# Hybrid mLSTM/Hyena block: step 0 of the MLP's first product is written between the last row tiles of the output projection

## The chip, the core and the metric

The kernel runs on one core of a Trainium2 chip. Its engines each follow their own instruction stream: TensorE (PE in the profile, matmuls and transposes), VectorE (DVE), ScalarE (ACT), GpSimd (POOL) and SyncE (SP, which here only starts DMA transfers). The time is that of one execution on the device in microseconds (us). For the kernel before it was measured three times: 2784.33, 2786.06 and 2790.24 us, median 2786.06.

## The reference

One encoder block over 2048 rows of width 1024. A mixing part (mLSTM heads and a Hyena operator) gives `y`, and then:

```python
x = x + rms_norm(y @ w_out, norm_mix_post)
hm = rms_norm(x, norm_mlp_pre)
ff = jnp.square(jax.nn.relu(hm @ w_mlp_in)) @ w_mlp_out
x = x + rms_norm(ff, norm_mlp_post)
```

`w_mlp_in` is 1024 x 4096 and `w_mlp_out` 4096 x 1024. Everything is float32.

## The kernel before

Only two stages matter here, the output projection and the first product of the MLP.

**Numbers in two parts.** A float32 operand of a matmul is held as a part hi, which ScalarE makes by a cast (L166), and a remainder lo, which VectorE or GpSimd makes by a subtraction (L169). One product of two operands takes three matmuls, hi and lo crossed (L159, L160, L161).

**The output projection** (`out_proj`, L1269) works on 16 row tiles of 128 rows in 18 turns of a loop. A turn i makes the operands of later row tiles, multiplies row tile i with `w_out` in two halves of 512 columns, and then runs `finish(i)`: the post norm (squares of `po` on ScalarE at L1198, the scaling on VectorE at L1204, the residual add on GpSimd at L1205), the store of the new rows, and the next norm (square L1333, root L1334, scale L1336). Two turns later `turn_out` transposes the normalized tile on TensorE (L1346), multiplies it with the norm's weight on VectorE (L1347), and stores what the MLP needs to DRAM (`ht`). For every second row tile GpSimd first forms the sums and differences of L1361 to L1364. Row tile 15 is thus finished in turn 15 and transposed in turn 17, the last.

**The first product of the MLP** (`up`, L1524) saves multiplications: a product of 2 x 2 blocks is computed with 7 smaller products instead of 8, from sums of blocks. The rows come in two halves, 0 (row tiles 0 to 7) and 1 (8 to 15), and the weights in 16 blocks, which gives 32 steps; steps 0 to 15 are half 0. A step computes its products in the order 1, 2, 6, 5, 7, 4, 3. Each is 12 matmuls (4 blocks of depth, three matmuls each), so a step is 84 matmuls, and ends in a PSUM bank, from which ScalarE copies it (product 1, L1561) or VectorE adds it up (L1539); relu and square are done on ScalarE (L1543, L1544) and results stored to DRAM (`ga`).

Product i of half h takes the operand `hm[i]`, which `right(h, i)` (L1470) loads from `ht` in two pieces of 512 KB, each split into hi and lo: the lo of the first piece is VectorE's, of the second GpSimd's. Weights of step s come from `up_weights(s)` (L1441): two loads, then four sums on GpSimd (L1452, L1453, L1456, L1458) with splits between them, whose hi parts are ScalarE's and lo parts GpSimd's. Operands 1 and 2 of half 0 and the weights of step 0 are prepared by `first_operands` during turns 11 to 14 and later of the output projection. Operands 6, 5, 7, 4 and 3 are loaded at the start of the MLP.

**What sets the order.** Inside the loop of the output projection and throughout the MLP, TensorE, VectorE and ScalarE follow the order of the code; GpSimd and SyncE are ordered by a scheduler within their dependencies. A tile of a pool waits for the last user of the place it takes. The pools of the output projection (`owp` with the weights `wo` and `wbo`, `owk` with its scratch) are closed after its last turn, and the pools of the MLP take their place.

A load goes through SyncE's queue and a store through ScalarE's, so that a store that waits for its data holds the ScalarE instructions behind it.

Of the kernel before, what the change touches and what calls it, by code (L numbers as in the profile page):

```python
# [17 lines left out]
D = 1024  # L18
# [129 lines left out]
class Builder:  # L148
# [95 lines left out]
    def build(self):  # L244
        tc, nc = self.tc, self.nc
        with ExitStack() as c:
# [66 lines left out]
            oc = ExitStack()  # L313
            out = self.out_proj(oc)
# [5 lines left out]
            self.hm_pool = {i: hp for i in (1, 2)}  # L320
# [4 lines left out]
            oc.close()  # L325
# [867 lines left out]
    def post(self, wk, src, wb, tmp, res, tag):  # L1193
# [8 lines left out]
        for e in range(2):  # L1202
            cs = slice(512 * e, 512 * e + 512)
            self.dve.scalar_tensor_tensor(tmp[e], src[e], r, wb[:, cs], ALU.mult, ALU.mult)  # L1204
            self.pool.tensor_tensor(res[:, cs], tmp[e], res[:, cs], ALU.add)  # L1205
# [63 lines left out]
    def out_proj(self, c):  # L1269
        tc, io = self.tc, self.io  # L1270
        pe, dve, act, pool = self.pe, self.dve, self.act, self.pool
        wp = c.enter_context(tc.tile_pool(name="owp", bufs=1))
        wk = c.enter_context(tc.tile_pool(name="owk", bufs=2))
        ps = c.enter_context(tc.tile_pool(name="opt", bufs=3, space=PSUM, side="right"))
        pp = c.enter_context(tc.tile_pool(name="opo", bufs=3, space=PSUM, side="right"))
        wo = [wp.tile([128, 8, D], F32R, name=f"wo{e}") for e in range(2)]
        wb = wp.tile([128, D], F32, name="wbo")
# [7 lines left out]
        def weight(k):  # L1285

            wf = ahead.pop(k)
            act.activation(wo[0][:, k, :], wf, AF.Copy, scale=yw[:, k:k + 1])
            dve.scalar_tensor_tensor(wo[1][:, k, :], wf, yw[:, k:k + 1], wo[0][:, k, :].bitcast(F32),
                                     ALU.mult, ALU.subtract)  # L1290
# [13 lines left out]
        def turned(src, tag):  # L1304
            y = [wk.tile([128, 4, 128], F32R, tag=f"{tag}{e}", name=f"{tag}{e}") for e in range(2)]
            self.turn_split(ps.tile([128, 512], F32, tag="tp", name="ptp", bufs=3), src, y)
            return y
# [10 lines left out]
        def part(po, e, y, k0):  # L1318
            cs = slice(512 * e, 512 * e + 512)
            for k in range(4):  # L1320
                self.mm3(po[e], (y[0][:, k, :], y[1][:, k, :]), (wo[0][:, k0 + k, cs], wo[1][:, k0 + k, cs]),
# [5 lines left out]
        def finish(h, po):  # L1327
            xt = wk.tile([128, D], F32, tag="xt", name="xt")
            self.load(xt, self.rows(io["x"][0], h))
            x1 = wk.tile([128, D], F32, tag="xo", name="xo", bufs=3)  # L1330
            self.post(wk, po, wb, (x1[:, 0:512], x1[:, 512:1024]), xt, "po")
            self.store(self.x1[h], xt)
            act.activation(x1, xt, AF.Square, accum_out=ss1[:, h:h + 1])  # L1333
# [46 lines left out]
        yz[1] = turned(zs.pop(1), "yhz")  # L1380
# [3 lines left out]
        ym = {0: turned(mixed(0), "yhm")}  # L1384
# [7 lines left out]
        for i in range(18):  # L1392
            with tc.manual_schedule(engines={mybir.EngineType.PE,mybir.EngineType.DVE,mybir.EngineType.Activation}):
                if i == 0:
# [3 lines left out]
                    ym[1] = turned(ys.pop(1), "yhm")  # L1398
# [3 lines left out]
                if 0 < i < 15:  # L1402
                    yz[i + 1] = turned(zs.pop(i + 1), "yhz")
# [7 lines left out]
                if 0 < i < 15:  # L1411
                    ym[i + 1] = turned(ys.pop(i + 1), "yhm")
# [80 lines left out]

    def mlp(self):
        tc, io = self.tc, self.io
        pe, dve, act, pool = self.pe, self.dve, self.act, self.pool
        with ExitStack() as c:
            hp = c.enter_context(tc.tile_pool(name="hmq", bufs=1))
            mk = self.mk = c.enter_context(tc.tile_pool(name="mmk", bufs=1))
            self.mwp = c.enter_context(tc.tile_pool(name="mwp", bufs=2))  # L1500
            ps = c.enter_context(tc.tile_pool(name="mlps", bufs=2, space=PSUM, side="right"))
            self.hm_pool.update({i: hp for i in (3, 4, 5, 6, 7)})
            self.wb2 = mk.tile([128, D], F32, name="wb2")
# [20 lines left out]
    def up(self, ring, next_bank, down):  # L1524
# [12 lines left out]

        def add(dst, a, b):
# [7 lines left out]
        w = self.w1_first  # L1546
        nxt = weights(1)
        for i in (6, 5, 7, 4, 3):
            self.right(0, i, staging, (None, pool))
        for s in range(n):  # L1550
            half, turn = s // 16, s == 15
            ga = self.ga[s % 16, half]
            gt = [ring((128, 2, 512), 0) for _ in range(2)]
            (c11, c12), (c21, c22) = [[t[:, b] for b in range(2)] for t in gt]
            for i in (1, 2, 6, 5, 7, 4, 3):
                pt = next_bank()
                hi, lo = self.hm[i]
                for k in range(4):
                    self.mm3(pt, w(i, k), (hi[:, k, :], lo[:, k, :]), k == 0, k == 3)
                if i == 1:  # L1560
                    act.copy(c11, pt)  # L1561
                elif i == 2:
                    p2 = pt
                    if s + 1 < n:
                        w1 = next(nxt)
                    if s + 2 < n:
                        nxt = weights(s + 2)
                elif i == 6:
                    add(c22, pt, c11)
                    add(c11, p2, c11)  # L1570
                    square(c11)
                elif i == 5:
                    add(c12, pt, c22)
                    p5 = pt
                elif i == 7:
                    add(c21, pt, c22)
                    add(c22, p5, c21)
                    square(c22)
                elif i == 4:
                    add(c21, pt, c21)  # L1580
                    square(c21)
                    self.store(ga[:, 2:4, :], gt[1])
                else:
# [234 lines left out]
```

## Time and profile before

| | |
|---|---|
| median of three runs | 2786.06 us (2784.33 to 2790.24) |
| profiled execution, its own time | 2789.98 us |
| its span, first to last instruction | 2787.9 us |
| mean granted clock of TensorE | 0.973 |
| last transposes of row tile 14 end | 1490.2 us after the span's start |
| first matmul of step 0 of the MLP | 1506.42 us |

A row of the timeline gives the start, the duration, the engine, the line and operation, what is written and read (tiles by their names), how many instructions the row holds, and in brackets how long the engine stood idle before it and what ended the wait. A row of waits gives engine, tile and line, what was waited for, the total, the count and the longest. A row of the windows gives for one stretch the busy time of each engine, the granted clock and the share of the DMA engines in use. A row of groups gives the busy time and mean duration of one kind of instruction.

### The profile page before, as it was taken

Reading aid. Unit: us, or ns where it says so; the run is one execution under the profiler, and the core shown is the slowest. Engines: PE = TensorE matmul, PEld = TensorE weight load, DVE = VectorE, ACT = ScalarE, POOL = GpSimd, SP = SyncE. Lnnn points to the kernel's source line nnn. Section 1 sums busy time; section 2 is a strip of 40 time slices with the busy share of each in tenths; the row PEclk is TensorE's granted clock in tenths of the full one; section 3 lists DMA queues with packets and bytes.
Section 4 is the critical chain, followed back from the end, with each engine's and each line's share of the span. In section 5 each row is a group of like instructions: output and inputs, shape, how many; then the busy total and the mean of one; then the engine's idle time right before and its main releaser. Section 6 shows DMA issues by size and latency. Waiting matters only on the chain. (4 is left out here: it accounts for less than half of the span.)

```text
span 2787.9 us, 35849 instructions
## 1 busy us (share of the span) xinstructions
PE 2617.9 (94%) x12422; PEld 2140.6 (77%) x12422; DVE 1530.7 (55%) x2593; ACT 1223.3 (44%) x2237; POOL 1199.6 (43%) x946
## 2 busy tenths in 40 slices
PE   6999999999899998888996999989999999999998
PEld 5778877777677888776775788868888888888876
DVE  5676643777436664664443454564445443443478
ACT  6355543655434444543332445455445233232244
POOL 1221124554215542424565877777774251310232
PEclk8999999999999999999998999989999999999999
DMA  6233346565556656955665444464445653444546
GB/s 168 61 99 106 106 138 201 183 194 169 189 192 176 186 164 227 267 187 187 212 214 198 143 159 143 156 223 141 157 159 201 222 181 114 113 144 153 194 152 226
DMA packets 307189, 474.24 MB, mean 170 GB/s; under 512 B 37814, under 2 KB 166198, under 8 KB 305984
## 3 DMA queue, kind: packets, MB, share of 16 engines
q1 hardware_dynamic: 231952, 333.24, 38.4%
q10 hardware_dynamic: 70304, 125.98, 12.1%
q0 software_dynamic: 4752, 12.72, 2.1%
q8 instruction: 99, 1.62, 0.2%
q14 instruction: 82, 0.67, 0.1%
HBM read 297.65 MB, written 174.20 MB: 169 GB/s over the span
## 5 line engine op out<-in xcount | busy, mean ns | idle before, releaser
L166 ACT CAST cb<-m 128x1024 fp32r<-128x1024 f32 (+1 forms) x346 | 281.8, 850 | 446.4 <-PE pm L159 385.7
L169 DVE TENSOR_TENSOR cb<-m,cb 128x1024 fp32r<-128x1024 f32 (+1 forms) x222 | 238.9, 1113 | 300.4 <-ACT cb L166 290.6
L159 PE MATMUL pm<-hm,cb 128*128 128x512 f32 x896 | 354.4, 396 | 15.0 <-issue 8.3
L160 PE MATMUL pm<-hm,cb 128*128 128x512 f32 x896 | 353.8, 395 | 13.3 <-POOL hm L169 9.6
L161 PE MATMUL pm<-hm,cb 128*128 128x512 f32 x896 | 352.4, 393 | 0.0
L160 PE MATMUL pm<-cb 128*128 128x512 f32 x880 | 343.9, 391 | 6.4 <-DVE cb L169 6.4
L159 PE MATMUL pm<-cb 128*128 128x512 f32 x880 | 342.7, 390 | 1.0 <-DVE cb L169 1.0
L161 PE MATMUL pm<-cb 128*128 128x512 f32 x880 | 343.1, 390 | 0.0
L169 POOL TENSOR_TENSOR cb<-m,cb 128x1024 fp32r<-128x1024 f32 x124 | 270.4, 2193 | 53.4 <-ACT cb L166 53.4
L1539 DVE TENSOR_TENSOR m<-pm,m 128x512 f32<-128x512 f32 x224 | 154.0, 690 | 243.3 <-PE pm L161 232.5
L159 PE MATMUL pt<-hn,w 128*128 128x512 f32 x640 | 270.9, 423 | 1.0 <-ACT hn L486 0.9
L169 POOL TENSOR_TENSOR raw<-raw,hi 128x512 fp32r<-128x512 f32 x160 | 205.4, 1296 | 129.5 <-ACT hi L166 118.3
L160 PE MATMUL pt<-hn,w 128*128 128x512 f32 x640 | 254.9, 398 | 0.3 <-DVE hn L487 0.2
L161 PE MATMUL pt<-hn,w 128*128 128x512 f32 x640 | 253.6, 396 | 0.0
L159 PEld LDWEIGHTS pm<-hm,cb 128*128 128x128 f32 x896 | 171.0, 191 | 53.2 <-issue 10.0
L160 PEld LDWEIGHTS pm<-hm,cb 128*128 128x128 f32 x896 | 171.0, 191 | 51.4 <-POOL hm L169 11.3
L160 PEld LDWEIGHTS pm<-cb 128*128 128x128 f32 x880 | 165.6, 188 | 43.8 <-DVE cb L169 9.4
L161 PEld LDWEIGHTS pm<-hm,cb 128*128 128x128 f32 x896 | 171.0, 191 | 35.5
L159 PEld LDWEIGHTS pm<-cb 128*128 128x128 f32 x880 | 165.4, 188 | 35.9 <-ACT junk L1728 1.4
L161 PEld LDWEIGHTS pm<-cb 128*128 128x128 f32 x880 | 165.6, 188 | 34.1
L1543 ACT ACTIVATE m<-m 128x512 f32<-128x512 f32 x128 | 80.5, 630 | 219.6 <-DVE m L1539 211.7
L630 POOL DMA_DIRECT2D vp<-vst x96 | 61.2, 642 | 236.4 <-ACT vst L626 235.1
(323 smaller groups left out, 5699.0 us busy)
## 6 DMA issues: line engine op xcount, KB each, us to landing
ga<-m ACTq DMA_DIRECT2D x96, 512.0 KB, 3.8
m<-ga SPq DMA_DIRECT2D x96, 512.0 KB, 3.7
d<-st ACTq DMA_DIRECT2D x64, 512.0 KB, 3.3
m<-in_w_mlp_in_dram SPq DMA_DIRECT2D x62, 512.0 KB, 4.6
m<-in_w_mlp_out_dram SPq DMA_DIRECT2D x114, 256.0 KB, 4.0
raw<-d SPq DMA_DIRECT2D x96, 256.0 KB, 2.8
xt<-in_x_dram SPq DMA_DIRECT2D x32, 512.0 KB, 5.6
dk<-kst SPq DMA_DIRECT2D x32, 512.0 KB, 3.3
```

Of the source, the lines that this page charges most:

```text
L159: pe.matmul(ps, w[1], x[0], start=first, stop=False)
L160: pe.matmul(ps, w[0], x[1], start=False, stop=False)
L161: pe.matmul(ps, w[0], x[0], start=False, stop=last)
L166: self.act.copy(hi, src)
L169: (eng_lo or self.dve).tensor_tensor(lo, src, hi.bitcast(F32), ALU.subtract)
L630: pool.dma_start(dst[:, 8 * b + e:8 * b + 8:2, cc:cc + 128], st[64 * e:64 * e + 64])
L1539: dve.tensor_tensor(dst, a, b, ALU.add)
L1543: act.activation(g, g, AF.Relu)
```

## The change

Four things are done. **One pool for both stages**: the pool `hmq` of the MLP's operands is opened before the output projection, whose weights take the places of operands 6, 5, 7 and 4, and whose turned tiles those of operand 3; `wbo` and `wb2`, the weights of the two post norms, share one place. The scratch pool is closed after turn 14, and a small pool `m0` takes its room. **Step 0 moves**: `first_step`, a generator, emits the loads of operands and the seven products of step 0 in turns 15 to 17; the code of a step is now `up_step`, and the MLP starts at step 1. **The norm of row tile 15**: `finish` is cut in two, `finish` and `normed`, so that operand loads can stand between them, and the residual add of row tile 15 is on VectorE instead of GpSimd. **Pools of the MLP** wait tile by tile for their places (`reuse_waits="tile"`).

```diff
+            self.hq = c.enter_context(tc.tile_pool(name="hmq", bufs=1))
+            self.hm_pool = {i: self.hq for i in range(3, 8)}
             out = self.out_proj(oc)
...
-            oc.close()
             self.mlp()
...
-            self.pool.tensor_tensor(res[:, cs], tmp[e], res[:, cs], ALU.add)
+            eng.tensor_tensor(res[:, cs], tmp[e], res[:, cs], ALU.add)
...
-        wp = c.enter_context(tc.tile_pool(name="owp", bufs=1))
-        wk = c.enter_context(tc.tile_pool(name="owk", bufs=2))
+        wp = self.hq
+        wl = c.enter_context(tc.tile_pool(name="owl", bufs=2))
+        gc = ExitStack()
+        wk = gc.enter_context(tc.tile_pool(name="owk", bufs=2))
...
-        wo = [wp.tile([128, 8, D], F32R, name=f"wo{e}") for e in range(2)]
-        wb = wp.tile([128, D], F32, name="wbo")
+
+        wos = {j: [wp.tile([128, 2, D], F32R, tag=f"hm{i}{e}", name=f"wo{e}") for e in range(2)]
+               for j, i in ((2, 6), (3, 5), (0, 7), (1, 4))}
+        wo = [[wos[k // 2][e][:, k % 2, :] for k in range(8)] for e in range(2)]
+        wb = wp.tile([128, D], F32, tag="wb", name="wbo")
...
-                if i < 16:
+                if i < 15:
                     part(pos[i], 1, ym[i], 0)
-                    xns[i] = finish(i, pos.pop(i))
-            if i > 10:
-                next(staged, None)
+                    xns[i] = normed(i, *finish(i, pos.pop(i)))
+                elif i == 15:
+
+                    part(pos[i], 1, ym[i], 0)
+                    step = self.first_step(c, pp)
+                    next(step)
+                    rows = finish(i, pos.pop(i))
+                    next(step)
+                    xns[i] = normed(i, *rows)
+                    next(step)
+                elif i == 16:
+                    for _ in range(4):
+                        next(step)
+                else:
+                    for _ in step:
+                        pass
+            if 10 < i < 15:
+                next(staged)
+            if i == 14:
+                gc.close()
             yield
-        for _ in staged:
-            pass
+        c.close()
...
+    def first_step(self, c, pp):
+
+        wk = c.enter_context(self.tc.tile_pool(name="m0", bufs=1))
+        count = [0]
+
+        def tile(shape, tag):
+            return wk.tile(list(shape), F32, tag=tag, name="m0", bufs={"g": 3, "s": 1, "r": 4}[tag])
+
+        def staging():
+            return tile((128, 2, 512), "r")
+
+        def bank():
+            count[0] += 1
+            if count[0] in (1, 2, 4, 5):
+                return self.h1p.tile([128, 512], F32, tag="h1", name="pm")
+            return pp.tile([128, 512], F32, tag="po", name="pm", bufs=3)
+
+        def then(i):
+            if i == 1:
+                self.right(0, 4, staging, (None, self.pool))
+            elif i == 2:
+                self.w1 = next(nxt)
+            elif i == 6:
+                self.right(0, 3, staging, (None, self.pool))
+
+        self.right(0, 6, staging, (None, self.pool))
+        yield
+        self.right(0, 5, staging, (None, self.pool))
+        yield
+        nxt = self.up_weights(1, [tile((128, 4, 256), "r") for _ in range(2)], tile((128, 2, 4, 128), "r"))
+        next(nxt)
+        self.right(0, 7, staging, (None, self.pool))
+        yield
+        yield from self.up_step(0, self.w1_first, lambda: tile((128, 2, 512), "g"), lambda: tile((128, 512), "s"), bank, then)
+
...
-            self.wb2 = mk.tile([128, D], F32, name="wb2")
+            self.wb2 = self.hq.tile([128, D], F32, tag="wb", name="wb2")
...
+        w1, nxt = self.w1, weights(2)
+        for s in range(1, n):
+            for _ in self.up_step(s, w1, lambda: ring((128, 2, 512), 0),
+                                  lambda: self.mk.tile([128, 512], F32, tag="mc", name="m4"), next_bank, then):
+                pass
```

How the order moves is seen at three places. In these rows `hm61` is the lo part of operand 6 and so on, `m` and `m0` are staging tiles and partial results, `cb` parts of weights, `pm` PSUM banks of products, `po` those of the output projection, `xo` and `xt` row tiles.

The first place is SyncE's queue after the last row tile of x has been asked for. Before:

```order
L231 DMA xt_14348<-in_x_dram 128x1x1024
L231 DMA wb2_14429<-in_norm_mlp_post_dram 128x1024
L231 DMA m_14431<-in_w_mlp_in_dram 128x4x256
L231 DMA m_14432<-in_w_mlp_in_dram 128x4x256
L231 DMA m_14438<-ht_84 128x1024
L231 DMA m_14442<-ht_84 128x1024
L231 DMA m_14448<-ht_84 128x1024
```

and of the changed kernel:

```order
L231 DMA xt_14325<-in_x_dram 128x1x1024
L231 DMA m0_14317<-ht_84 128x1024
L231 DMA m0_14321<-ht_84 128x1024
L231 DMA m0_14344<-ht_84 128x1024
L231 DMA m0_14348<-ht_84 128x1024
L231 DMA m0_14356<-in_w_mlp_in_dram 128x4x256
L231 DMA m0_14357<-in_w_mlp_in_dram 128x4x256
L231 DMA wb2_14586<-in_norm_mlp_post_dram 128x1024
L231 DMA m0_14363<-ht_84 128x1024
L231 DMA m0_14367<-ht_84 128x1024
L231 DMA m0_14406<-ht_84 128x1024
L231 DMA m0_14410<-ht_84 128x1024
```

The four loads of operands 6 and 5 moved ahead of the weights of step 1 and of wb2, whose place is that of `wbo`; those of 7 and 4 stand behind them.

The second place is VectorE from the post norm of row tile 15 to the first evacuation of step 0. Before:

```order
L1204 SCALAR_TENSOR_TENSOR xo_14350<-po1_14276,po_r_14358,wbo_12116 128x512
L1335 RECIPROCAL r1_12118<-ss1_12117 128x1
L1336 TENSOR_SCALAR xo_14350<-xt_14348,r1_12118 128x1024
L1347 TENSOR_TENSOR xo_14350<-pto_14389,nw1_3589 128x512
L1347 TENSOR_TENSOR xo_14350<-pto_14395,nw1_3589 128x512
L169 TENSOR_TENSOR hm61_14437<-m_14438,hm60_14436 128x1024
L169 TENSOR_TENSOR hm51_14447<-m_14448,hm50_14446 128x1024
L169 TENSOR_TENSOR hm71_14457<-m_14458,hm70_14456 128x1024
L169 TENSOR_TENSOR hm41_14467<-m_14468,hm40_14466 128x1024
L169 TENSOR_TENSOR hm31_14477<-m_14478,hm30_14476 128x1024
L1539 TENSOR_TENSOR m_14487<-pm_14539,m_14486 128x512
```

and of the changed kernel (L1205 is the scaling, L1206 the residual add, L1347 to L1359 the norm of row tile 15, L1625 the evacuation adds):

```order
L1205 SCALAR_TENSOR_TENSOR xo_14327<-po1_14240,po_r_14335,wbo_12125 128x512
L1206 TENSOR_TENSOR xt_14325<-xo_14327,xt_14325 128x512
L169 TENSOR_TENSOR hm51_14343<-m0_14344,hm50_14342 128x1024
L1347 RECIPROCAL r1_12127<-ss1_12126 128x1
L1348 TENSOR_SCALAR xo_14327<-xt_14325,r1_12127 128x1024
L1359 TENSOR_TENSOR xo_14327<-pto_14490,nw1_3589 128x512
L1359 TENSOR_TENSOR xo_14327<-pto_14496,nw1_3589 128x512
L169 TENSOR_TENSOR hm71_14362<-m0_14363,hm70_14361 128x1024
L169 TENSOR_TENSOR hm41_14405<-m0_14406,hm40_14404 128x1024
L1625 TENSOR_TENSOR m0_14389<-pm_14446,m0_14388 128x512
L1625 TENSOR_TENSOR m0_14388<-pm_14414,m0_14388 128x512
L1625 TENSOR_TENSOR m0_14389<-pm_14513,m0_14389 128x512
```

The splits of operands 6 (further up) and 5 moved between the pieces of row tile 15; those of 7 and 4 stand behind its last multiply and ahead of the first adds that empty banks.

The third place is ScalarE between steps 1 and 2. Before:

```order
L1561 COPY m_14629<-pm_14631 128x512
L234 DMA ga_85<-m_14487 128x1024
L234 DMA ga_85<-m_14486 128x1024
L234 DMA ga_85<-m_14620 128x1024
L234 DMA ga_85<-m4_14621 128x512
L166 CAST cb_14658<-m_14534 128x1024
L1543 ACTIVATE m_14629<-m_14629 128x512
L166 CAST cb_14660<-m_14535 128x1024
L1544 ACTIVATE m_14629<-m_14629 128x512
```

and of the changed kernel (L1638 is the copy of product 1, L1629 and L1630 relu and square):

```order
L1638 COPY m_14593<-pm_14595 128x512
L1629 ACTIVATE m_14593<-m_14593 128x512
L1630 ACTIVATE m_14593<-m_14593 128x512
L1629 ACTIVATE m_14594<-m_14594 128x512
L1630 ACTIVATE m_14594<-m_14594 128x512
L1629 ACTIVATE m_14593<-m_14593 128x512
L1629 ACTIVATE m_14594<-m_14594 128x512
L166 CAST cb_14622<-m_14588 128x1024
L1630 ACTIVATE m_14594<-m_14594 128x512
L166 CAST cb_14624<-m_14589 128x1024
```

The copy in both is product 1 of step 1, the first cast in both the first of step 2's weights. It moved from ahead of the relus and squares of step 1 to behind all but the last squares.

More of the change, by code (lines that the diff above doesn't have):

```diff
@@ L1536, in weights, with then, up_step @@
             return g
+        def then(i):
+            nonlocal nxt, w1
+            if i == 2:
+                if s + 1 < n:
+                    w1 = next(nxt)
+                if s + 2 < n:
+                    nxt = weights(s + 2)
+            if s == 15:
+                self.right(1, i, staging, (None, pool if i in (2, 7, 3) else None))
+            if s == n - 1 and i in (2, 7):
+                next(down)
+        w1, nxt = self.w1, weights(2)
[3 more added lines that the diff above has]
+                pass
+    def up_step(self, s, w, pair, single, next_bank, then):
+        pe, dve, act, pool = self.pe, self.dve, self.act, self.pool
+        ga = self.ga[s % 16, s // 16]
+        gt = [pair() for _ in range(2)]
+        (c11, c12), (c21, c22) = [[t[:, b] for b in range(2)] for t in gt]
         def add(dst, a, b):
@@ L1544, in square @@
             act.activation(g, g, AF.Square)
[L1546 to L1583, printed above, removed]
-                    add(c12, pt, c12)
-                    square(c12)
-                    st, s4 = ring((128, 2, 512), 0), self.mk.tile([128, 512], F32, tag="mc", name="m4")
-                    add(st[:, 0], c12, c22)
-                    dve.tensor_tensor(c12, c11, c12, ALU.subtract)
-                    dve.tensor_tensor(st[:, 1], st[:, 0], c11, ALU.subtract)
-                    dve.tensor_tensor(s4, c21, st[:, 1], ALU.subtract)
-                    self.store(ga[:, 0:2, :], gt[0])
-                    self.store(ga[:, 4:6, :], st)
-                    self.store(ga[:, 6, :], s4)
-                if turn:
-                    self.right(1, i, staging, (None, pool if i in (2, 7, 3) else None))
-                if s == n - 1 and i in (2, 7):
-                    next(down)
-            w = w1
@@ new lines, in up_step @@
+        for i in (1, 2, 6, 5, 7, 4, 3):
+            pt = next_bank()
+            hi, lo = self.hm[i]
+            for k in range(4):
+                self.mm3(pt, w(i, k), (hi[:, k, :], lo[:, k, :]), k == 0, k == 3)
+            if i == 1:
+                act.copy(c11, pt)
+            elif i == 2:
+                p2 = pt
+            elif i == 6:
+                add(c22, pt, c11)
+                add(c11, p2, c11)
+                square(c11)
+            elif i == 5:
+                add(c12, pt, c22)
+                p5 = pt
+            elif i == 7:
+                add(c21, pt, c22)
+                add(c22, p5, c21)
+                square(c22)
+            elif i == 4:
+                add(c21, pt, c21)
+                square(c21)
+                self.store(ga[:, 2:4, :], gt[1])
+            else:
+                add(c12, pt, c12)
+                square(c12)
+                st, s4 = pair(), single()
+                add(st[:, 0], c12, c22)
+                dve.tensor_tensor(c12, c11, c12, ALU.subtract)
+                dve.tensor_tensor(st[:, 1], st[:, 0], c11, ALU.subtract)
+                dve.tensor_tensor(s4, c21, st[:, 1], ALU.subtract)
+                self.store(ga[:, 0:2, :], gt[0])
+                self.store(ga[:, 4:6, :], st)
+                self.store(ga[:, 6, :], s4)
+            then(i)
+            yield
```

42 lines of the change are left out of this document (22 added, 20 removed).

## The prediction

> **What bounds the kernel now.** I read the page's busy times and its chain first, then TensorE's longest waits between the last tiles of the output projection and the MLP, then windows of that stretch, then its rows.
>
> ```profile
> span 2787.9 us, 35849 instructions
> PE 2617.9 (94%) x12422; PEld 2140.6 (77%) x12422; DVE 1530.7 (55%) x2593; ACT 1223.3 (44%) x2237; POOL 1199.6 (43%) x946
> ```
>
> ```profile
> PE pto L1346 <- DVE xo L1336: 13.3, 1, 13.3
> PE pm L159 <- issue: 8.3, 1, 8.3
> PE pm L159 <- ACT hm L166: 2.8, 1, 2.8
> ```
>
> ```profile
> core 0: us, PE busy (x) PEld busy (x) DVE busy (x) ACT busy (x) POOL busy (x), PEclk, DMA share, GB/s
> 1490.20:1503.50 13.30, 0.01 (x1) 0.03 (x1) 3.56 (x8) 3.00 (x8) 6.18 (x5) 0.65 0.58 178
> 1514.50:1522.60 8.10, 0.00 (x0) 0.00 (x0) 0.00 (x0) 1.04 (x1) 0.00 (x0) 0.72 1.01 343
> 1538.50:1556.00 17.50, 15.46 (x50) 11.62 (x51) 8.51 (x10) 9.69 (x16) 17.42 (x10) 0.71 0.28 88
> ```
>
> TensorE (PE) is busy 94% of the span, so a change that only reorders work can win only where PE stands or runs slowly. One such place is here. From 1490.20, after the transposes of row tile 14, PE waits 13.3 us for row tile 15 to be normalized. In the second window nothing computes and the DMA engines are full: the loads of the operands for products 6, 5, 7, 4 and 3. In the third PE has work but the granted clock is 0.71 and VectorE (DVE) and ScalarE (ACT) are half idle, while GpSimd (POOL) is busy 17.42 of 17.50 us: step 1's weights are late.
>
> Now the size of what can be won.
>
> ```profile
> 1609.00 0.59 ACT L1561 COPY m<-pm 128x512 f32<-128x512 f32 x1 [0.70 <-PE pm L161]
> ```
>
> ```profile
> 1628.04 0.59 ACT L1561 COPY m<-pm 128x512 f32<-128x512 f32 x1 [0.70 <-PE pm L161]
> ```
>
> ```profile
> 1439.43 0.77 PE L159 MATMUL po<-wo,yhz 128*128 128x512 f32 x1 [1.96 <-DVE xo L1204]
> 1440.00 0.63 PE L160 MATMUL po<-wo,yhz 128*128 128x512 f32 x1
> 1440.43 0.63 PE L161 MATMUL po<-wo,yhz 128*128 128x512 f32 x1
> ```
>
> ```profile
> 1506.42 0.77 PE L159 MATMUL pm<-hm,cb 128*128 128x512 f32 x1 [0.98 <-DVE xo L1347]
> ```
>
> The two copies evacuate product 1 of steps 4 and 5. A step of 84 matmuls takes 1628.04 − 1609.00 = 19.04 us, 0.2267 us a matmul. Counting back from 1609.00 over a hand-off (some 0.2), product 1 (12 × 0.2267 = 2.72) and one step, step 3 starts at **1587.0**; another step back, step 2 at 1568.0. After a pause, even one of 1.96 us, matmuls start 0.43 us apart; ten of those cost 10 × (0.43 − 0.2267), about 2.1 us a restart. Step 0 begins at 1506.42, when row 15's transposes are done. From 1490.2 to 1587.0 are 96.8 us, three steps are 57.1 and the transposes of row 15 about 2: **some 38 us** are pauses and slow clock. The change can win only from those, since rows from step 3 on stand in the same order on each engine.
>
> **The change part by part.** It puts step 0 into the last three turns. Products 1 and 2 fill part of the 13.3 us; 6 and 5 follow before row 15's transposes, then 7, 4, 3. No matmul is added or removed. What counts is when operands, evacuations and weights come. I walk the new order with durations of before.
>
> *Operands 6 and 5, row 15.* ScalarE is free at 1495.05, because the stores of row tile 13's sums stand ahead on its queue:
>
> ```profile
> 1493.30 1.36 ACTq L234 DMA_DIRECT2D ht<-tb  x2
> 1495.05 0.60 ACT L1198 ACTIVATE xo<-po 128x512 f32<-128x512 f32 x1 [7.91 <-issue]
> ...
> 1500.84 1.06 ACT L1333 ACTIVATE xo<-xt 128x1024 f32<-128x1024 f32 x1 [4.00 <-POOL xt L1205]
> ...
> 1521.51 2.21 ACT L166 CAST hm<-m 128x1024 fp32r<-128x1024 f32 x2 [19.20 <-DMA m<-ht]
> ```
>
> ```profile
> 1497.12 1.41 DVE L1204 SCALAR_TENSOR_TENSOR xo<-po,po_r,wbo 128x512 f32<-128x512 f32 x2
> 1522.65 1.23 DVE L169 TENSOR_TENSOR hm<-m,hm 128x1024 fp32r<-128x1024 f32 x1 [16.48 <-ACT hm L166]
> ```
>
> Operand 6's two casts (2.1) now stand ahead of row 15's squares, so the squares begin at 1497.15; squares, sum and root take 1497.12 − 1495.05 = 2.07, to 1499.2. The two scalings (0.7 each) and, now on DVE, the two residual adds (0.69 each by L1539, the evacuation adds in the groups below, the nearest DVE adds of 512 columns; 1.55 by L1591, beside POOL; POOL has only operand 6's split then, so I take 0.69 and keep +1.7) end at 1502.1. Operand 5's casts follow (1504.6), then row 15's second square, root and scale, 2.5 us (1500.84 to 1503.50, the end of the 13.3 us wait): 1507.3. PE ends product 5 at about 1509.2 and the transposes with their multiplies at 1511.5, where before they ended at 1506.4. Row 15 is thus 5 us late; by itself that costs nothing, since half 1, which needs it, starts at step 16.
>
> *The added wait.* Operands 7 and 4 do not get the free early load that 6 and 5 get. The staging pool has four buffers, and SyncE's queue holds the two weight loads and then wb2, whose place is still read by row 15's scaling until 1502. The first load for 7 waits for a staging buffer that DVE's split of operand 5 frees at 1504.9. Behind it the queue is a chain: load, cast, split on DVE or POOL, next load. The price of a load:
>
> ```profile
> 1386.02 0.34 SPq L231 DMA_DIRECT2D hr<-ht  x1
> ```
>
> ```profile
> 1390.25 1.04 ACT L166 CAST hm<-hr 128x1024 fp32r<-128x1024 f32 x1
> ```
>
> ```profile
> m<-ht SPq DMA_DIRECT2D x10, 512.0 KB, 9.1
> ```
>
> 4.2 us alone, 9.1 with ten queued together. Here one or two are in flight, so I take 4.2. Operand 7 is there at 1509.1 but its split on DVE stands behind row 15's multiplies (1511.5): 1512.7. That frees the buffer for operand 4: load 1517.0, cast 1518.1, split 1519.3. Only then come the two evacuation adds (0.69 each) that free product 2's bank for product 7: **1520.8**. PE has stood since 1510.2, 10.6 us. That is the new form of the 8.3 us wait.
>
> *Step 1's weights.* Products 7 and 4 take 24 × 0.2267 and a restart, to 1528.3. Next on PE is step 1's product 5, which stands between products 4 and 3 of step 0 and needs POOL.
>
> ```profile
> L169 POOL TENSOR_TENSOR cb<-m,cb 128x1024 fp32r<-128x1024 f32 x27 | 66.6, 2467 | 10.2 <-ACT cb L166 10.2
> ...
> L1539 DVE TENSOR_TENSOR m<-pm,m 128x512 f32<-128x512 f32 x62 | 42.3, 690 | 62.6 <-PE pm L161 59.7 <-DMA ga<-m 2.3
> ...
> L1453 POOL TENSOR_TENSOR m<-m 128x512 f32<-128x512 f32 x10 | 15.5, 1554 | 0.8
> L1452 POOL TENSOR_TENSOR m<-m 128x512 f32<-128x512 f32 x10 | 15.1, 1506 | 19.1 <-DMA m<-in_w_mlp_in_dram 9.9 <-issue 9.2
> L169 POOL TENSOR_TENSOR hm<-m,hm 128x1024 fp32r<-128x1024 f32 x5 | 14.7, 2943 | 13.4 <-DMA m<-ht 13.3
> L1456 POOL TENSOR_TENSOR m<-m 128x512 f32<-128x512 f32 x10 | 13.8, 1378 | 0.0
> L1591 DVE TENSOR_TENSOR m<-m 128x512 f32<-128x512 f32 x8 | 12.4, 1550 | 0.3
> L1458 POOL TENSOR_TENSOR m<-m 128x512 f32<-128x512 f32 x9 | 11.6, 1291 | 0.6
> ...
> L169 DVE TENSOR_TENSOR hm<-m,hm 128x1024 fp32r<-128x1024 f32 x5 | 11.5, 2322 | 23.4 <-ACT hm L166 23.4
> L169 POOL TENSOR_TENSOR cb<-m,cb 128x512 fp32r<-128x512 f32 x8 | 10.4, 1298 | 0.0
> ...
> L1362 POOL TENSOR_TENSOR tb<-xo 128x512 f32<-128x512 f32 x3 | 3.8, 1279 | 8.7 <-issue 5.0 <-DVE xo L1347 3.6
> ```
>
> Operand 7's second piece is loaded once POOL has split that of 5 (1507.3), cast when the store of row 15's transposes ahead of it on ACT's queue has gone (1513.1), and split on POOL by 1515.5 (2.4, as for weights; 2.94 in the mean of the operands). The second piece of 4 loads (1519.8) and is cast (1520.9); POOL, held by one sum placed ahead, starts its split then and ends it at 1523.3. Then two sums, two splits, a sum and a split: 1.55 + 1.38 + 2.47 + 2.47 + 1.29 + 2.47 = 11.6, to 1534.9. PE stands 6 us. Product 3 then waits for POOL's split of operand 3, behind three sums of row 15 and a split of 512 columns: 3 × 1.28 + 1.30 + 2.47 = 7.6, 1542.5. With its last 6 matmuls (1.4) and the evacuation that frees a bank (0.69 and 0.25 to hand over), the other 72 matmuls of step 1 run from 1544.9 to **1561.2**. Before, step 1 ended at 1568.0, so up to here 6.8 us are won.
>
> *Step 2's weights.* Before, the first cast of step 2's weights came ahead of step 1's squares:
>
> ```profile
> 1553.99 6.13 ACTq L234 DMA_DIRECT2D ga<-m  x4
> 1560.22 1.05 ACT L166 CAST cb<-m 128x1024 fp32r<-128x1024 f32 x1 [5.79 <-DVE m L1591]
> ```
>
> Now it stands behind all but one of them, so it waits for the evacuation of step 1's last product. After PE's end at 1561.2 come three DVE adds (0.25 to hand over, 2 × 0.69), a square (0.6, as at 1495.05), the cast (1.05), POOL's split (2.47) and 0.5 of hand-offs: 6.2; and 1.0 more because ACT's queue, held by four stores that wait for DVE's subtractions, lags. Step 2 starts at 1561.2 + 7.3 = **1568.5**, no earlier than before (1568.0). After 24 matmuls and a restart (1576.0) its product 6 needs POOL's split, sum, sum, sum, sum, split: 2.47 + 1.51 + 1.29 + 1.55 + 1.38 + 2.47 = 10.7 after 1568.5, 1579.2. PE stands 3.2 us, restarts again, and step 3 starts at 1579.2 + 60 × 0.2267 + 2.1 = **1594.9**.
>
> The sum: 1594.9 − 1587.0 is **+8 us**. The profiled execution, 2789.98 us (span 2787.9 and 2.1 around it), would become 2798; it lies 3.9 above the median of the three runs, 2786.06, so the forecast for the median is **2794**.
>
> Two rules against rows. Several short pauses in place of one long one cost more restarts: the row at 1439.43 shows slow matmuls after only 1.96 us. The Trainium skill (TensorE: Matmul & The Clock Gate, section "What's actually happening") states that the clock halves after an idle window of about 3.4 us that runs freely; by that the three longer of my pauses (10.6, 6, 7.3) would surely cost a restart and the one of 3.2 us perhaps none, which would give 2.1 less, 2792. The trace differs, since 1.96 us were enough there, so I count all four.
>
> The splits on DVE average 2.32 us here where the one at 1522.65, with POOL idle, took 1.23. The Trainium skill (SBUF — State Buffer, section "SBUF: two separate sides") has DVE instructions with two inputs in SBUF and POOL instructions lock one port pair against each other, which agrees; by it the residual adds moved to DVE and the split of operand 4 could each wait for a whole POOL split, and the estimate would be 2.5 us higher.
>
> **The rivals.** *The late pauses are hidden* (18%): the casts for step 2 reach ACT early enough, because DVE and ACT keep up with PE. Against it: the cast follows a square that needs the last product. Without the 7.3 and 3.2, 10.5 us less: 2783.5, within 0.2% of before.
>
> *Step 0 simply moves up* (12%): it starts 1506.4 − 1490.2 = 16.2 us earlier and everything behind it is stretched as before; 2770, faster. For it speaks that operands 6 and 5 are loaded free in the shadow of row 14; against it, that operands 7 and 4 need row 15's place on SyncE's queue and DVE.
>
> *Loads at the loaded price* (7%): the legs for 7 and 4 take 9.1 instead of 4.2, because stores of x and of the operands run beside them. Two legs in chain, 9.8 us: 2804, slower. It decides if these loads take over 4.2 each; the second piece of 4 shows it first. My forecast (63%) itself is on the slower side; the mechanism that ends on the other side is the second rival.
>
> That the change does not do what it says is excluded: the rows of the new order show step 0's products ahead of row 15's transposes.
>
> **How the numbers follow.** A measurement of this kernel can tell about 0.2%, 5.6 us, from no change. The forecast's own range is +4 to +14, by the add's +1.7, loads up to 2 us longer, and a restart less; about an eighth of it lies within 5.6. Slower: 0.63 × 0.87 + 0.07 + 0.02 = 0.64. Same: 0.08 + 0.14 of the first rival = 0.22. Faster: 0.12 + 0.02 = 0.14. The range 2780 to 2804 holds the forecast, the first rival and half of the third; it leaves out the second.
>
> **What would show it.** Right: product 7 of step 0 starts near 1521 after a pause of about 10 us, released by DVE; step 1's product 5 waits some 6 us for POOL; step 2's first matmul waits 6 to 8 us for POOL's split with the cast behind a square; step 3's product 1 starts near 1595. Wrong: step 2 follows step 1 without a pause (first rival), product 7 is at work before 1512 (second), or the loads for 7 take over 8 us (third). A change of the clock or the pace of matmuls anywhere after step 3 would lie outside all of this.

## The result and the profile after

The changed kernel takes **2795.74 us** (median of six runs, 2794.08 to 2798.89), the kernel before, with three more runs beside it, 2783.42 us (2780.83 to 2790.24). The ratio is 1.0040, interval 1.0028 to 1.0051: slower by 12 us, where 8 were forecast. The forecast started from 2786.06, the median of three runs; the six of before lie lower.

The profiled execution took 2798.89 us, its span is 2797.1, 9.2 us more than before. Where they come from is read from a few landmarks on ScalarE. The first rows, from the timeline of the changed kernel, are the square of row tile 14 and the copies of product 1 in steps 6, 7 and 14:

```profile
1483.26 1.06 ACT L1345 ACTIVATE xo<-xt 128x1024 f32<-128x1024 f32 x1 [4.07 <-POOL xt L1206]
...
1655.11 0.59 ACT L1638 COPY m<-pm 128x512 f32<-128x512 f32 x1 [0.71 <-PE pm L161]
...
1674.24 0.59 ACT L1638 COPY m<-pm 128x512 f32<-128x512 f32 x1 [0.71 <-PE pm L161]
...
1808.12 0.59 ACT L1638 COPY m<-pm 128x512 f32<-128x512 f32 x1 [0.71 <-PE pm L161]
```

and the same places before:

```profile
1485.66 1.06 ACT L1333 ACTIVATE xo<-xt 128x1024 f32<-128x1024 f32 x1 [4.05 <-POOL xt L1205]
...
1647.08 0.59 ACT L1561 COPY m<-pm 128x512 f32<-128x512 f32 x1 [0.70 <-PE pm L161]
...
1666.12 0.59 ACT L1561 COPY m<-pm 128x512 f32<-128x512 f32 x1 [0.70 <-PE pm L161]
...
1799.40 0.59 ACT L1561 COPY m<-pm 128x512 f32<-128x512 f32 x1 [0.70 <-PE pm L161]
```

The changed profile reaches the square 2.4 us *earlier*, ahead of anything that the change moves; such offsets differ from run to run (in the experiments below the square lies between 1478.3 and 1487.0). From the square to step 6 it takes 1655.11 − 1483.26 = 171.85 us, before 161.42: **10.4 us** are lost in this stretch, which I call the stretch from here on. From step 7 to step 14 it takes 133.88 against 133.28 us: in calm steps, without any wait, each step takes 19.13 instead of 19.04. That is a second, small loss, which the prediction didn't have.

TensorE's waits in the stretch, the changed kernel; compare with those that the prediction shows of before:

```profile
PE pm L159 <- POOL cb L169: 15.4, 3, 6.1
PE pm L159 <- DVE m L1625: 10.4, 2, 9.7
PE pm L159 <- ACT hm L166: 4.0, 2, 3.5
PE pm L160 <- POOL hm L169: 2.4, 2, 1.8
```

The wait of 13.3 us for row 15 and that of 8.3 for the operands are gone. In their place stand one of 9.7 us for VectorE and three for GpSimd's weights. On the timeline of TensorE (rows that end a wait):

```profile
1502.12 0.74 PE L159 MATMUL pm<-hm,cb 128*128 128x512 f32 x1 [3.51 <-ACT hm L166]
...
1519.32 0.77 PE L159 MATMUL pm<-hm,cb 128*128 128x512 f32 x1 [9.66 <-DVE m L1625]
...
1532.69 0.80 PE L159 MATMUL pm<-hm,cb 128*128 128x512 f32 x1 [6.08 <-POOL cb L169]
...
1540.96 0.50 PE L160 MATMUL pm<-hm,cb 128*128 128x512 f32 x1 [1.81 <-POOL hm L169]
...
1543.18 0.80 PE L159 MATMUL pm<-hm,cb 128*128 128x512 f32 x1 [0.78 <-DVE m L1625]
...
1566.86 0.79 PE L159 MATMUL pm<-hm,cb 128*128 128x512 f32 x1 [5.41 <-POOL cb L169]
...
1578.23 0.80 PE L159 MATMUL pm<-hm,cb 128*128 128x512 f32 x1 [3.96 <-POOL cb L169]
```

These are, in order, product 5 and product 7 of step 0, product 5 of step 1, the second half of product 3, the other products of step 1, step 2, and step 2's product 6. And the reason for the last two, on ScalarE and GpSimd:

```profile
1562.21 1.23 ACT L1629 ACTIVATE m<-m 128x512 f32<-128x512 f32 x2 [2.32 <-DVE m L1625]
1563.35 1.03 ACT L166 CAST cb<-m 128x1024 fp32r<-128x1024 f32 x1
```

```profile
1564.45 4.68 POOL L169 TENSOR_TENSOR cb<-m,cb 128x1024 fp32r<-128x1024 f32 x2 [15.49 <-ACT cb L166]
```

GpSimd stands 15.49 us for a cast that ScalarE could have made (1.03 us), but which stands behind relus that wait for step 1's last products.

**A correction.** The part on the kernel before says that ScalarE, VectorE and TensorE follow the order of the code throughout the MLP. That holds only in the loop of the output projection. In the MLP all engines are ordered by the scheduler: in the code, the casts of step 2's weights are written right behind product 2 of step 1, and only the scheduler put them behind the squares. The walk of the prediction went by the order as it came out, so its numbers aren't touched, but the remedy is simpler than it looked.

### The profile page after: what moved, and what is told of

Its sections match the earlier page's. It is cut to its first block, busy times and chain, and to the rows that moved or that the text cites. A ratio compares the mean times of both kernels' runs of the same rounds, so it can differ in the third digit from the quotient of the medians.

```text
span 2797.1 us, 35830 instructions
## 1 busy us (share of the span) xinstructions
PE 2623.2 (94%) x12422; PEld 2142.3 (77%) x12422; DVE 1529.3 (55%) x2595; ACT 1223.3 (44%) x2237; POOL 1198.4 (43%) x944
## 5 line engine op out<-in xcount | busy, mean ns | idle before, releaser
L1625 DVE TENSOR_TENSOR m<-pm,m 128x512 f32<-128x512 f32 x224 | 154.2, 690 | 255.8 <-PE pm L161 240.9
L1629 ACT ACTIVATE m<-m 128x512 f32<-128x512 f32 x128 | 80.6, 631 | 239.5 <-DVE m L1625 231.7
```

The source lines that it names most:

```text
L1625: dve.tensor_tensor(dst, a, b, ALU.add)
L1629: act.activation(g, g, AF.Relu)
```

## The experiments

All times are medians, with the kernel before beside them on the same chip; the chips differ between experiments, so that versions are compared by their ratios to before. "Stretch" is from the square of row tile 14 to the copy of step 6's product 1 in the profiled execution, "calm" the time from step 7's copy to step 14's.

| | median | before beside it | ratio (95%) | stretch | calm |
|---|---|---|---|---|---|
| before | 2783.42 | | | 161.42 | 133.28 |
| changed kernel | 2795.74 | 2783.42 | 1.0040 (1.0028 to 1.0051) | 171.85 | 133.88 |
| e1 casts first | 2783.98 | 2786.91 | 0.9994 (0.9983 to 1.0004) | 155.00 | 133.89 |
| e2 split of 4 on GpSimd | 2797.16 | 2786.91 | 1.0042 (1.0030 to 1.0054) | 170.88 | 133.89 |
| e3 add on GpSimd | 2797.56 | 2786.91 | 1.0044 (1.0032 to 1.0056) | 170.08 | 133.89 |
| e4 before, casts late | 2797.29 | 2786.91 | 1.0047 (1.0034 to 1.0060) | 172.52 | 133.28 |
| e5 small tiles elsewhere | 2795.63 | 2784.07 | 1.0045 (1.0032 to 1.0058) | 170.78 | 133.28 |
| e6 fifth staging buffer | 2790.10 | 2784.07 | 1.0021 (1.0012 to 1.0030) | 163.83 | 133.89 |
| e7 casts first, small tiles | 2778.31 | 2784.07 | 0.9980 (0.9972 to 0.9989) | 157.11 | 133.28 |
| e8 all three | 2778.47 | 2784.07 | 0.9979 (0.9970 to 0.9988) | 154.39 | 133.28 |
| e9 as e7, products late | 2780.49 | 2784.39 | 0.9993 (0.9984 to 1.0002) | 158.20 | 133.28 |
| e10 as e8, split 4 later | 2776.84 | 2784.39 | 0.9973 (0.9962 to 0.9983) | 155.98 | 133.17 |

**e1: are the late casts the loss?** ScalarE follows the code in steps 1 and 2.

```diff
-            for _ in self.up_step(s, w1, ...):
-                pass
+            with self.tc.manual_schedule(engines={mybir.EngineType.Activation}) if s < 3 else ExitStack():
+                for _ in self.up_step(s, w1, ...):
+                    pass
```

> The changed kernel, with ScalarE in the order of the code during steps 1 and 2 of the MLP, so that the casts of step 2's weights stand right behind the copy of step 1's product 1, ahead of step 1's relus and squares; nothing else. Theory (the casts held behind the squares cost the two late pauses, 5.4 and 4.0 us, and the slow restarts behind them): both pauses are gone, step 2 follows step 1 without one, and the time falls by 13 to 16 us against the changed kernel, to 5 to 7 us below the kernel before or at least level with it. Rival (GpSimd is the limit there and would be late anyway, since it does 15.4 us of sums and splits for these weights): the pauses stay within 3 us of what they were, and the time is still 9 or more above before.

The stretch falls by 16.85 us, and the time from 1.0040 of before to 0.9994, 12.8 us. TensorE's waits from 1480 to 1610 us in e1 hold only one for weights, step 1's; step 2 starts without a pause:

```profile
PE pm L159 <- DVE m L1626: 10.4, 2, 9.7
PE pm L159 <- POOL cb L169: 5.1, 1, 5.1
PE pm L159 <- ACT hm L166: 4.0, 2, 3.5
```

On ScalarE the three casts stand right behind the copy:

```profile
1551.56 0.59 ACT L1639 COPY m<-pm 128x512 f32<-128x512 f32 x1 [3.62 <-DVE m L1665]
1552.04 2.94 ACT L166 CAST cb<-m 128x1024 fp32r<-128x1024 f32 x3
```

The time falls a little less than the 13 to 16 us of the theory, but its mechanism holds, since both late pauses are gone. The rival falls: GpSimd isn't the limit. That e1 is faster than before isn't shown by its interval, though its stretch is 6.4 us shorter.

**e4: does the place of the casts cost as much without the change?** The kernel before, step 2's weights written behind step 1's last product, ScalarE in the order of the code in that step.

```diff
                 elif i == 2:
                     p2 = pt
-                    if s + 1 < n:
-                        w1 = next(nxt)
...
+                if s == 1 and i == 3:
+                    if s + 1 < n:
+                        w1 = next(nxt)
```

> The kernel before, without the change, where in step 1 of the MLP only the preparation of step 2's weights is written behind the last product and ScalarE keeps the order of the code in that step, so that the casts stand behind the squares as in the changed kernel. Theory (the place of these casts is the loss, whatever the change did ahead of it): step 2 waits 8 to 10 us for GpSimd's split, and the time is 9 to 14 us above before, about as much as the changed kernel. Rival (the changed kernel loses by its late operands, and the place of the casts is harmless where everything else is in time): less than 3 us above before.

It is 1.0047 of before, 11.1 us more in the stretch, as much as the changed kernel loses. One row of TensorE carries it, the start of step 2:

```profile
1574.19 0.79 PE L159 MATMUL pm<-hm,cb 128*128 128x512 f32 x1 [8.80 <-POOL cb L169]
```

The casts stand somewhat later here than in the changed kernel, behind three stores as well: the first begins 5.3 us after TensorE's last matmul, there 1.9 us. That the two kernels lose nearly the same is therefore in part chance. Still, with e1 this settles the larger loss: the late place of four casts is enough to make a kernel this much slower, without anything that step 0 does.

**e2: is the longest pause the costly one?** The 9.7 us ahead of product 7 are due to VectorE's split of operand 4.

```diff
-                self.right(0, 4, staging, (None, self.pool))
+                self.right(0, 4, staging, (self.pool, self.pool))
```

> The changed kernel, with the lo part of operand 4's first piece made on GpSimd instead of VectorE, so that VectorE reaches the two adds that free the bank of product 7 earlier. Theory (what binds is the chain on GpSimd to step 1's weights, and the pause of 9.7 us ahead of product 7 is only where TensorE happens to stand): the pause ahead of product 7 falls to under 2 us, TensorE waits longer later, step 1's product 5 starts no earlier than 1532.5 and the whole takes 0 to 3 us more than the changed kernel. Rival (the longest pause is what costs): the time falls by 6 to 8 us.

Product 7 starts 9 us earlier, at 1509.97, and the time is the same as the changed kernel's. The wait has moved to step 1's product 5:

```profile
1509.97 0.51 PE L159 MATMUL pm<-hm,cb 128*128 128x512 f32 x1 [0.18 <-ACT hm L166]
...
1533.76 0.80 PE L159 MATMUL pm<-hm,cb 128*128 128x512 f32 x1 [8.07 <-POOL cb L169]
```

A pause of 9.7 us is removed and nothing is won, because GpSimd's weights end last. The edit also gives GpSimd one split more to do ahead of them, so that e2 alone doesn't settle it; e10 below removes a pause at this place without that.

**e3: the residual add.**

```diff
-            self.post(wl, po, wb, ..., "po", dve if h == 15 else pool)
+            self.post(wl, po, wb, ..., "po", pool)
```

> The changed kernel, with the residual add of row tile 15 back on GpSimd as before the change. Theory (row tile 15 is only a small part of the chain): the two adds take 2.5 us there instead of 1.4 on VectorE, and the time moves by -0.5 to +1 us against the changed kernel. Rival (the adds on VectorE collide with GpSimd's split of operand 6 and hold row tile 15 up): it falls by 2.5 us or more.

No difference that the runs show (1.0044). The stretch is 1.8 us shorter in the one profile, where the theory allowed 0.5. TensorE's start of step 1 came at half pace in the changed kernel and at full pace in e3, behind the same pause (more in the last section), which is worth 1.6 us of it:

```profile
1541.69 0.50 PE L159 MATMUL pm<-hm,cb 128*128 128x512 f32 x1 [0.78 <-DVE m L1625]
```

Neither engine is a bad place for the add. In the changed kernel it took what the walk gave it:

```profile
1498.54 0.69 DVE L1206 TENSOR_TENSOR xt<-xo,xt 128x512 f32<-128x512 f32 x1
```

**e6: the chain of loads.** Five staging buffers instead of four; the last result tile of step 0 takes one of them.

```diff
-            return wk.tile(list(shape), F32, tag=tag, name="m0", bufs={"g": 3, "s": 1, "r": 4}[tag])
+            return wk.tile(list(shape), F32, tag=tag, name="m0", bufs={"g": 2, "s": 1, "r": 5}[tag])
...
+        def pair():
+            pairs[0] += 1
+            return tile((128, 2, 512), "g" if pairs[0] < 3 else "r")
```

> The changed kernel, with five staging buffers for the loads of step 0 instead of four (the last result tile of step 0 takes one of them instead of one of its own). Theory (the chain load, cast, split, next load holds operands 7 and 4 and step 1's weights, because there are four buffers): the pause ahead of product 7 falls from 9.7 to about 7 us and that ahead of step 1's product 5 from 6.1 to about 4, and step 1's other products start 5 to 6 us earlier; the pauses in step 2 stay as they are, so the time falls by 4 to 6 us against the changed kernel. Rival (SyncE's wb2, or row 15 on VectorE, holds those loads): the pauses stay within 1 us and the time is the same.

The pause ahead of product 7 falls to 5.3 us, that ahead of step 1's product 5 hardly (5.5), and both come earlier. The stretch is 8.0 us shorter and the ratio goes from 1.0040 to 1.0021, by some 5 us; of the pauses in step 2 the first is the same. Rows of TensorE:

```profile
1515.54 0.77 PE L159 MATMUL pm<-hm,cb 128*128 128x512 f32 x1 [5.29 <-DVE m L1631]
...
1528.51 0.80 PE L159 MATMUL pm<-hm,cb 128*128 128x512 f32 x1 [5.54 <-POOL cb L169]
...
1561.11 0.79 PE L159 MATMUL pm<-hm,cb 128*128 128x512 f32 x1 [5.41 <-POOL cb L169]
```

So four buffers did hold operands and weights back, as the prediction's chain had it. With the fifth the first load of operand 7 starts at 1498.31, ahead of that of wb2 on SyncE's queue:

```profile
1498.31 0.34 SPq L231 DMA_DIRECT2D m<-ht  x1
```

Nor was it wb2 that held the loads: in the changed kernel SyncE had issued it at 1499.92 and started the loads of operand 7 at 1503.35, when VectorE had split the first piece of operand 5 (1502.10 and 1.22 us):

```profile
1499.92 0.34 SPq L231 DMA_DIRECT2D wb<-in_norm_mlp_post_dram  x1
1503.35 23.70 SPq L231 DMA_DIRECT2D m<-ht  x6
```

```profile
1502.10 1.22 DVE L169 TENSOR_TENSOR hm<-m,hm 128x1024 fp32r<-128x1024 f32 x1 [1.48 <-ACT hm L166]
```

**e5: the slower calm steps.** Product 3 of step 6 begins and ends, in the changed kernel, with

```profile
1687.64 0.40 PE L159 MATMUL pm<-hm,cb 128*128 128x512 f32 x1
...
1690.43 0.39 PE L159 MATMUL pm<-hm,cb 128*128 128x512 f32 x1
```

and before with

```profile
1679.52 0.39 PE L159 MATMUL pm<-hm,cb 128*128 128x512 f32 x1
...
1682.24 0.39 PE L159 MATMUL pm<-hm,cb 128*128 128x512 f32 x1
```

(the second row of each is the first matmul behind it): 2.79 against 2.72 us for 12 matmuls; the other six products take 2.72 to 2.74. The granted clock is 1.00 in both, so it isn't the clock. In the shared pool two small tiles of the norm come ahead of operand 3's places.

```diff
-        ss1 = wp.tile([128, 16], F32, name="ss1")
-        r1 = wp.tile([128, 16], F32, name="r1")
+        ss1 = wl.tile([128, 16], F32, name="ss1", bufs=1)
+        r1 = wl.tile([128, 16], F32, name="r1", bufs=1)
```

> The changed kernel, with the two tiles ss1 and r1 (16 numbers a partition each) taken out of the shared pool hmq and put into another pool, so that the places of operand 3 behind them lie 128 bytes a partition elsewhere; the order is that of the changed kernel. In the traces a steady step takes 19.13 us in the changed kernel and 19.04 in the one before, and the excess lies in product 3 alone (2.79 against 2.72 us). Theory (operand 3, which lies behind those tiles, is read more slowly because of where it lies): product 3 takes 2.72 us, a step 19.04, and over some 28 steps the time falls by 2 to 3 us against the changed kernel. Rival (product 3 is slower for another reason of the shared pool, such as its neighbours): a step stays at 19.13 and the time is the same.

In the trace the theory holds: the calm steps are back at 133.28 us and each product at 2.72. The time doesn't show it: 1.0045 of before, where the changed kernel had 1.0040, and intervals of 0.25% don't tell 2 or 3 us apart. That the place of these two tiles, and with it that of operand 3 behind them, sets product 3's pace is shown; what about the place does is not.

**e7 and e8: what is left when the losses are taken out.** e7 is e1 and e5 together, e8 has the fifth buffer as well.

> The casts of step 2's weights first, and ss1 and r1 out of the shared pool, together. Theory: both gains add up, 13 to 17 and 2 to 3 us, so that the time is 15 to 20 us below the changed kernel and 5 to 8 below the kernel before. Rival (one of them is taken back by the other): less than 3 us below before.

> As the run before it, and with the fifth staging buffer. Theory: the early pauses shrink by about 5 us, but with step 1 that early GpSimd is late with step 2's weights by about 2.5 us, so that 1 to 4 us more are won: 6 to 12 us below the kernel before. Rival (GpSimd takes all of it back): no more than 1 us below the run with casts and small tiles.

e7 is 0.9980 of before, 5.8 us faster, within the range of the theory. e8 is no faster (0.9979), less than its theory said, which gave 1 to 4 us more; by the times its rival holds. In its profile the stretch is 2.7 us shorter, and 4.1 if it is taken to step 7's copy (ScalarE was late with step 6's), but the runs don't show it.

**e9: what do the early products bring?** e7 with step 0's products behind row 15's transposes, where they were before; the early loads stay.

```diff
-                elif i == 16:
-                    for _ in range(4):
-                        next(step)
-                else:
+                elif i == 17:
                     for _ in step:
                         pass
```

> As the run with the casts of step 2 first and the small tiles elsewhere (2778.3 us against 2784.1 before), but the products of step 0 are all written behind row 15's transposes, as before the change; the shared pool and the early loads of operands 6 and 5 stay. Theory (early products gain little, since operands 7, 4 and 3 and step 1's weights come when they come): TensorE again waits some 14 to 16 us for row 15, but has fewer pauses behind it, and the time is 2 to 5 us more than in that run, still 0 to 4 below before. Rival (the early products are what the change gains): the 13 to 16 us by which step 0 begins earlier are lost, and the time is over 8 us more than in that run.

2.2 us more than e7, on another chip; 0.9993 of before. TensorE waits

```profile
PE pto L1358 <- DVE xo L1348: 18.3, 1, 18.3
PE pm L159 <- ACT hm L166: 11.1, 1, 11.1
```

The second wait is for operand 3, whose casts on ScalarE come only behind the last cast of step 1's weights, and that waited for GpSimd's sum:

```profile
1537.39 0.62 ACT L166 CAST cb<-m 128x512 fp32r<-128x512 f32 x1 [4.22 <-POOL m L1483]
```

The stretch is only 1.1 us longer than e7's. So the products between the last row tiles, taken by themselves, bring 1 us by the stretch and 2 to 4 by the times, which the intervals don't separate; two long waits do nearly as well as several short ones.

**e10: once more the pause ahead of product 7**, now with everything else mended: in e8, VectorE's split of operand 4 is moved behind the two adds. `later` only notes the subtraction, which is then issued after product 6.

```diff
             if i == 1:
-                self.right(0, 4, staging, (None, self.pool))
+                self.right(0, 4, staging, (later, self.pool))
...
             elif i == 6:
+                for a in later.todo:
+                    self.dve.tensor_tensor(*a)
```

> As the run with all three edits (2778.5 us), and VectorE makes the lo part of operand 4's first piece behind the two adds that free the bank of product 7, not ahead of them. Theory (as with the split on GpSimd: the pause ahead of product 7 does not bind, the weights do): that pause goes from 6.1 to under 2 us, the wait for step 1's weights grows by about as much, and the time moves by no more than 2 us either way. Rival (with five buffers that pause binds): 3 to 5 us less.

That pause is gone; in its place TensorE waits 4.1 us inside product 4 and 5.8 for step 1's weights:

```profile
1520.31 0.80 PE L160 MATMUL pm<-hm,cb 128*128 128x512 f32 x1 [4.10 <-POOL hm L169]
1528.59 0.79 PE L159 MATMUL pm<-hm,cb 128*128 128x512 f32 x1 [5.78 <-POOL cb L169]
```

2776.84 us, 1.6 less than e8 on another chip, which the intervals don't separate. By its median it is the fastest version: 0.9973 of before (0.9962 to 0.9983).

## Why the prediction was right

The walk, point by point. The changed profile is 2.4 us ahead where the walk begins, so 2.4 is taken off each forecast:

| | forecast | measured | pause forecast | measured |
|---|---|---|---|---|
| product 7 of step 0 | 1518.4 | 1519.32 | 10.6 | 9.66 |
| step 1's product 5 | 1532.5 | 1532.69 | 6 (6.6 by its sum) | 6.08 |
| the rest of step 1 | 1542.5 | 1543.18 | | 0.78 |
| step 2 | 1566.1 | 1566.86 | 7.3 | 5.41 |
| its product 6 | 1576.8 | 1578.23 | 3.2 | 3.96 |
| step 3 | 1592.5 | 1594.8 | | |

(step 3 from its copy at 1597.73, less 2.72 and 0.2.) The releasers are those that were named: VectorE's adds, GpSimd's weights, and for step 2 the late cast. That cast waits for the relus of step 1's last two results (1.23 us), where the walk had one square (0.6).

- **The gain taken back.** Step 0 began at 1487.57 instead of 1506.42, yet step 2 no earlier than before. Right, and e2, e9 and e10 show why: GpSimd's weights end last, wherever TensorE waits (in e9 through the casts behind them).
- **The late casts.** Right, shown from both sides by e1 (taken out) and e4 (put into the kernel before). The pause itself was 1.9 us shorter than forecast, 1.0 of it because the extra lag of ScalarE didn't come; a restart at half pace in step 1 (1.6 us), which the walk had left out, happened to make up for it.
- **The added wait of operands 7 and 4.** Its mechanism was right in the four buffers (e6); the place of wb2 on SyncE's queue, named beside them, held nothing.
- **The size.** 10.4 us in the stretch against 8. Of the 2.4 between, 0.8 were there when step 2 began, by small misses of either sign. Behind it GpSimd's sums for step 2, 1.7 us each where the walk had 1.3 to 1.55, bring 0.7, and the restart at product 6 cost 2.9 us (14 matmuls in 6.04 us, at full pace 3.17), not 2.1, which brings 0.8. A restart has no one price: the row at 1439.43, from which the walk took 2.1, cost 1.7 itself, and the one of step 2 cost 1.8. What was missed altogether is the slower product 3, 0.09 us a step. That the median, 2795.74, lies only 1.7 us from the 2794 is luck: the kernel before came out 2.6 us below the 2786.06 to which the 8 were added, and the change costs 12.3.
- **The rivals.** Late pauses hidden: no, both are there. Step 0 simply moves up: no; e8 comes nearest, and its stretch is 7.0 us shorter than before's. Loads at the loaded price: no. The first load of operand 7, issued at 1503.35, ended ScalarE's wait at 1508.29, 4.9 us, not 9.1, and the second piece of operand 4, which the prediction named as the first to show it, took 3.7:

```profile
1508.29 1.05 ACT L166 CAST hm<-m 128x1024 fp32r<-128x1024 f32 x1 [3.90 <-DMA m<-ht]
```

```profile
1514.65 0.32 SPq L231 DMA_DIRECT2D m<-ht  x1
```

```profile
1518.34 1.04 ACT L166 CAST hm<-m 128x1024 fp32r<-128x1024 f32 x1 [1.74 <-DMA m<-ht]
```

- **The two rules.** The residual adds took 0.69 us each and the split of operand 4 1.23, so no lock held them in this run. But GpSimd stood idle beside them (from 1497.12 to 1503.09 and from 1514.63 to 1517.93), so the run doesn't test the lock. Half pace came behind all four pauses, as the walk counted them, behind the 3.96 us too, for which the rule that the prediction quotes from the Trainium skill had left it open (TensorE: Matmul & The Clock Gate, section "What's actually happening"). By an estimate from that section's 3.4 us, only a pause over 6.8 us surely holds a whole window, so the prediction's "surely" was too strong for the pause of 6. More on restarts below.

## What to carry to other kernels

When work is moved ahead to fill a wait, follow the last operand that it needs, and the engine that prepares the step behind it: here the matmuls had 13 us to fill and the weights for the next step came when they came. A pause is worth what ends later because of it; two of 9.7 and 6.1 us were taken away with no gain that the runs show (e2, e10). And a scheduler that sees a new program may order a quite different place anew: four casts for a later step cost more than the whole change could bring, and naming their order brought it back.

## What was not expected of the hardware

**An operand's place changes the pace of matmuls.** 12 matmuls took 2.79 us instead of 2.72 with the same shapes, no wait and a granted clock of 1.00, and 2.72 again when two small tiles were taken from ahead of the operand (e5). The seven calm steps take 133.88 or 133.89 us in every run with those tiles there (the changed kernel, e1, e2, e3, e6), and 133.17 to 133.28 in every other.

**The same pause may or may not cost a restart.** Behind the wait of 0.78 us, step 1 starts at half pace in the changed kernel,

```profile
1543.78 0.63 PE L160 MATMUL pm<-hm,cb 128*128 128x512 f32 x1
```

and in e1, behind the same wait, at full pace:

```profile
1540.32 0.50 PE L160 MATMUL pm<-hm,cb 128*128 128x512 f32 x1 [0.93 <-POOL hm L169]
...
1542.53 0.50 PE L159 MATMUL pm<-hm,cb 128*128 128x512 f32 x1 [0.78 <-DVE m L1626]
1542.87 0.40 PE L160 MATMUL pm<-hm,cb 128*128 128x512 f32 x1
```

From the first matmul to the tenth are 3.74 us in the one and 2.17 in the other. The pauses ahead of it differ: 1.81 us at 1540.96 in the changed kernel, 0.93 at the same place in e1. The other runs agree: ahead of the same 0.78 us, 1.80 (e5) and 1.78 (e7) go with half pace, and 0.99 (e3), 1.05 (e8), 1.52 (e10) and 1.60 (e6) with full pace. In e7 half pace sets in one matmul later:

```profile
1536.76 0.50 PE L160 MATMUL pm<-hm,cb 128*128 128x512 f32 x1 [1.78 <-POOL hm L169]
...
1538.99 0.51 PE L159 MATMUL pm<-hm,cb 128*128 128x512 f32 x1 [0.78 <-DVE m L1626]
1539.33 0.60 PE L160 MATMUL pm<-hm,cb 128*128 128x512 f32 x1
```

So what stood idle shortly ahead counts too. The Trainium skill (TensorE: Matmul & The Clock Gate, section "What's actually happening") says that the clock is set by how busy the engine was in a window that runs freely; that agrees with a pause of 0.78 us counting once and not another time, and not with a pause having a price of its own, as the walk had it. The idle window of about 3.4 us that the Trainium skill gives there as the condition for the slow clock is not borne out: the two pauses of 1.81 and 0.78 us together are shorter. What exactly the condition is stays open.
